# Six gate projections per layer as pairs by seven block products, and keys, queries and first transposes placed earlier, in a two-layer hybrid attention trunk

## The chip, the cores and the metric

The kernel runs on one core of a Trainium2 chip, in one launch. The metric is device time in microseconds (us) of one execution; lower is better. Three runs of the kernel before gave a median of 852.07 us (850.96 to 852.84). The profile used below is one further execution of the same program.

## The reference

The input is one sequence of 512 positions with 1024 channels, in fp32. Two layers follow each other; each computes

```
h = x @ w_in                      # 5024 columns: latents, gates, Diff q/k/v, merge gates
A: latent attention, 8 heads      # softmax(q k^T) v, times SiLU(gate_A), @ w_branch_a -> y_a
B: differential attention, 4 heads# (softmax1 - lam*softmax2) v, RMSNorm, times SiLU(gate_B), @ w_branch_b -> y_b
g = sigmoid(gates + b_merge)      # 2 x 1024 columns of h
merged = g[:, :1024] * y_a + g[:, 1024:] * y_b
x = LayerNorm(alpha * x + merged @ w_out)
```

So every layer has 16 merge gates of 128 columns each: eight for branch A and eight for branch B. A gate needs a product of a 128x1024 block of transposed weights with the whole transposed input (1024x512).

## The kernel before

**Layout and precision.** Almost everything is kept feature-major: 128 channels on the partitions, the 512 positions along the free axis. The input of a layer lies in SBUF as xH and xL: the value rounded to the matmul's format fp32r, and the remainder. Each weight tile is split likewise (`slot`, lines 109 to 116): one DMA of 128x1024 into a `wr` buffer, a cast on ACT to `wh` (line 112), and two subtractions on DVE to `wl` (line 115). A product of full precision is then three matmuls (`mm3`, lines 125 to 128): high by high, high by low, low by high. A projection (`proj`) is 8 blocks along the contraction, 24 matmuls of 512 columns in all, into one PSUM bank.

**Order of the work in a layer.** First come the latents and norms, then branch A's values (VS), then the eight heads of branch A. A head computes four blocks of scores (`mla_scores`), each followed on DVE by a row maximum (line 172) and on ACT by the exponential (line 174). The values of a head (`mla_values`) follow while the next head's scores run: `keyT` transposes a block of probabilities on PE (line 181, four matmuls against the identity), ACT casts the result from PSUM (line 183), DVE subtracts to get the low part (line 184), and two matmuls add to the output in the bank `pv` (lines 365, 366). `weave` alternates the two generators. Between heads stand `keys`, `query` and the projections of a table (`fill`, then `dfill` for branch B): SiLU gates, Diff q and k, Diff v. The four heads of branch B run in the same way. After the last matmul of a head's values comes a short chain: ACT copies the output to `op` (line 470), PE transposes it (line 476), ACT squares and sums it (line 479), two small DVE instructions (lines 481 and 482) prepare the variance, GpSimd raises it to the power -1/2 (line 484). The next step of that generator (the tail) broadcasts the result over the partitions by four transposes on PE (line 143, in `bcast`); DVE multiplies (lines 487, 488), and `split` makes the two parts of yB in `lat` buffers (lines 162, 163).

**The merge stage.** The eight A gates and A branch products are spread over heads 0 to 2 of branch B (`g` and `m` in `dfill`). After head 3 stand gate B0, the tail of head 3, and then four times two B gates and two B branch products (lines 590 to 601), and the output projection.

**What sets the order.** The kernel is written in program order, and a scheduler then places each engine's instructions by its own estimate of when each can start, so PE, ACT, DVE and the SP queue hold an order that mixes neighbouring steps. Every engine, and the SP queue that issues nearly all loads, works through its own list in that order. Buffers come from rings: two `wr`, three each of `wh` and `wl`, eight `p` (probabilities, and raw tiles), eight `y` (parts of yA), sixteen `qm`, two `op`, four `pt`, six `kv`. A write into a ring's buffer waits for the last reader of what lay there.

## Time and profile before

| what | value |
|---|---|
| median of three runs | 852.07 us (850.96 to 852.84) |
| the profiled execution, its own time | 851.0 us |
| span from its first to its last instruction | 849.1 us |
| granted TensorE clock, mean | 0.997 |
| PE busy | 837.6 us, 99% |
| DVE busy | 587.8 us, 69% |
| ACT busy | 428.0 us, 50% |
| GpSimd busy | 22.7 us, 3% |

PE is the matmul record, PEld the weight loads that run beside it. Matmul records overlap: one begins before the last has left the array, so that the distance from one start to the next, not the recorded duration, is what a matmul takes of PE's time. A row of the timeline reads: start in us, duration in us, engine, source line, operation, output and inputs, shape, count, and in brackets the idle time before it with what ended that.

### The profile page before, as it was taken

The page shows a single profiled execution, that of the slowest core. Times are in us where ns is not written, and L with a number is a line of the kernel's source. Part 1 is how long each engine was busy: PE and PEld are TensorE (multiplying, and loading weights), DVE is VectorE, ACT ScalarE, POOL GpSimd, SP SyncE. Part 2 cuts the span into 40 slices and gives each one's busy share as a digit, 9 for nine tenths or more (in the row PEclk, how much of TensorE's full clock was granted, in tenths as well). Part 3 has the DMA queues.
Part 4 walks back from the last instruction along what each step waited for, and adds up shares of the span by engine and source line. Part 5 has one row for each costly group of instructions (what it writes and reads, how often), then busy time and mean ns, then how long its engine had stood idle before and what let it go on. Part 6 is the DMA issues. An engine that isn't in the chain of part 4 may idle for free.

```text
span 849.1 us, 11080 instructions
## 1 busy us (share of the span) xinstructions
PE 837.6 (99%) x4143; PEld 695.7 (82%) x4143; DVE 587.8 (69%) x1070; ACT 428.0 (50%) x842; POOL 22.7 (3%) x30
## 2 busy tenths in 40 slices
PE   8999999999999999999999999999999999999996
PEld 7877877878898888888897778788788888888885
DVE  6789988586646845455867899877667566545457
ACT  5767775463544633332336777755546354433310
POOL 0100000000000000000120000000000000000001
PEclk9999999999999999999999999999999999999998
DMA  8311011213222452223532110112222233432322
GB/s 305 118 44 38 32 51 50 74 36 102 87 75 75 124 173 86 93 95 119 185 110 70 39 37 26 50 53 72 76 75 75 79 96 123 155 97 96 100 75 99
DMA packets 27702, 75.70 MB, mean 89 GB/s; under 512 B 3201, under 2 KB 7809, under 8 KB 27649
## 3 DMA queue, kind: packets, MB, share of 16 engines
q1 hardware_dynamic: 27504, 74.74, 27.7%
q8 instruction: 32, 0.52, 0.3%
q10 hardware_dynamic: 144, 0.26, 0.1%
q14 instruction: 22, 0.17, 0.1%
HBM read 70.80 MB, written 4.19 MB: 88 GB/s over the span
## 4 chain that ended last, share of the span: by engine, by line
PE 88%; ACT 5%; DVE 4%; DMA 2%; issue 1%; SPq 0%; POOL 0%; DVEq 0%; ACTq 0%
PE psacc L126 22%; PE psacc L127 22%; PE psacc L128 22%; PE pstr L181 4%; PE pspv L365 2%; PE pssc L126 2%; PE pssc L127 2%; PE pssc L128 2%; PE pspv L126 2%; PE pspv L366 2%; PE pspv L127 1%; PE pspv L128 1%; DMA wr<-in_wts_dram 1%; ACT wh L112 1%; PE pssc L444 1%; PE pssc L448 1%
## 5 line engine op out<-in xcount | busy, mean ns | idle before, releaser
L115 DVE TENSOR_TENSOR wl<-wr,wh 128x512 fp32r<-128x512 f32 x192 | 127.3, 686 | 145.6 <-ACT wh L112 145.2
L126 PE MATMUL psacc<-xH,wh 128*128 128x512 f32 x496 | 195.1, 393 | 0.0
L127 PE MATMUL psacc<-xL,wh 128*128 128x512 f32 x496 | 194.4, 392 | 0.0
L128 PE MATMUL psacc<-xH,wl 128*128 128x512 f32 x496 | 193.9, 391 | 0.0
L112 ACT CAST wh<-wr 128x1024 fp32r<-128x1024 f32 x96 | 101.0, 1052 | 175.0 <-PE psacc L127 115.5
L126 PEld LDWEIGHTS psacc<-xH,wh 128*128 128x128 f32 x496 | 93.2, 188 | 18.9
L127 PEld LDWEIGHTS psacc<-xL,wh 128*128 128x128 f32 x496 | 93.2, 188 | 18.4
L128 PEld LDWEIGHTS psacc<-xH,wl 128*128 128x128 f32 x496 | 93.2, 188 | 18.4
L174 ACT ACTIVATE p<-pssc,sm 128x512 f32<-128x512 f32 x128 | 88.2, 690 | 27.9 <-DVE sm L172 27.4
L172 DVE TENSOR_REDUCE sm<-pssc 128x1 f32<-128x512 f32 x128 | 86.7, 683 | 4.8 <-PE pssc L128 2.4
L183 ACT CAST pt<-pstr 128x512 fp32r<-128x512 f32 x96 | 55.6, 586 | 28.2 <-PE pstr L181 27.9
L184 DVE TENSOR_TENSOR pt<-pstr,pt 128x512 fp32r<-128x512 f32 x96 | 64.7, 685 | 7.1 <-ACT pt L183 6.3
L181 PE MATMUL pstr<-ident,p 128*128 128x128 f32 x384 | 57.3, 272 | 0.1
L181 PEld LDWEIGHTS pstr<-ident,p 128*128 128x128 f32 x384 | 47.3, 140 | 11.8 <-ACT p L174 0.5
L126 PE MATMUL psacc<-wh,xH 128*128 128x256 f32 x128 | 36.3, 284 | 0.0
L127 PE MATMUL psacc<-wl,xH 128*128 128x256 f32 x128 | 36.3, 284 | 0.0
L128 PE MATMUL psacc<-wh,xL 128*128 128x256 f32 x128 | 36.2, 283 | 0.0
L365 PE MATMUL pspv<-pt,vs 128*128 128x512 f32 x64 | 29.1, 455 | 0.4
L126 PE MATMUL pssc<-kv,qm 128*128 128x512 f32 x64 | 26.7, 423 | 0.9 <-ACT kv L306 0.6
L126 PE MATMUL psacc<-y,wh 128*128 128x512 f32 x64 | 25.5, 399 | 0.0
L366 PE MATMUL pspv<-pt,vs 128*128 128x512 f32 x64 | 25.5, 399 | 0.0
L127 PE MATMUL pssc<-kv,qm 128*128 128x512 f32 x64 | 25.3, 396 | 0.0
(296 smaller groups left out, 1591.6 us busy)
## 6 DMA issues: line engine op xcount, KB each, us to landing
wr<-in_wts_dram SPq DMA_DIRECT2D x106, 512.0 KB, 3.6
qr<-in_wts_dram SPq DMA_DIRECT2D x16, 128.0 KB, 2.1
p<-in_gb_dram SPq DMA_DIRECT2D x8, 256.0 KB, 2.9
y<-in_x_dram SPq DMA_DIRECT2D x8, 256.0 KB, 5.3
x_scratch<-y SPq DMA_DIRECT2D x8, 256.0 KB, 2.1
y<-x_scratch SPq DMA_DIRECT2D x8, 256.0 KB, 5.3
out_dram<-y SPq DMA_DIRECT2D x8, 256.0 KB, 2.0
p<-in_xT_dram SPq DMA_DIRECT2D x7, 256.0 KB, 4.9
```

The lines of the kernel that those rows point to most:

```text
L112: nc.scalar.copy(hi, raw)
L115: nc.vector.tensor_tensor(lo[:, c], raw[:, c], fr(hi[:, c]), ALU.subtract)
L126: nc.tensor.matmul(o, lhsT=lh, rhs=rh, start=start, stop=False)
L127: nc.tensor.matmul(o, lhsT=lh, rhs=rl, start=False, stop=False)
L128: nc.tensor.matmul(o, lhsT=ll, rhs=rh, start=False, stop=stop)
L172: nc.vector.tensor_reduce(m, S, axis=AX.X, op=ALU.max, negate=True)
L174: nc.scalar.activation(p, S, AF.Exp, bias=m, scale=1.0, accum_out=sums)
L181: nc.tensor.transpose(b[:, t * P:(t + 1) * P], pts[t][:, c * P:(c + 1) * P], ident)
L183: nc.scalar.copy(h, b)
L184: nc.vector.tensor_tensor(lo, b, fr(h), ALU.subtract)
L365: nc.tensor.matmul(pv, lhsT=v, rhs=ph, start=kc == 0, stop=False)
L366: nc.tensor.matmul(pv, lhsT=v, rhs=pl, start=False, stop=kc == NT - 1)
```

## The change

**Keys, queries and first transposes.** `mla_values` and `diff_values` gain a step at their start: the first `keyT` is issued, then the generator yields. The main loops take that step right after the scores of the head, ahead of `fill` and `dfill`. `keys` and `query` move from the start of a round to just after its `weave`, one head further ahead. The small computation of lambda moves from before the heads to behind the first scores.

**Gates B2 to B7.** They become three pairs, (2,3), (4,5) and (6,7). A pair is a product of a 256x1024 weight block with the 1024x512 input, cut into 2x2 blocks (128 by 512, and 512 by 256), and computed by seven block products with sums, in place of eight. A block product is 12 matmuls of 256 columns (`product`). The sums of the input's blocks are made once a layer on GpSimd (`x_forms`, four steps `x0` to `x3` in `dfill`), written to a DRAM tile `xf` by eight DMAs of GpSimd's queue, and loaded as four 128x1024 tiles through the `wr` ring (`y0` to `y3`, at the end of `dfill[2]`); each is split on ACT and DVE into two `y` or two `qm` pairs. The sums of the weights' blocks are four additions of 128x512 per pair on GpSimd (`add`), from four raw loads of 128x512 into `p` buffers; seven forms are split, each with a cast on ACT and a subtraction on DVE. `tc.issue_after` keeps the sums behind the latest power on GpSimd's list. Seven results are combined from PSUM by four ACT copies and three DVE additions of 256 columns, and the tanh moves behind these. The branch B products use the `sc` banks.

**The start.** Six instead of seven warming matmuls; the first block of the input is loaded in two pieces, both from SP's queue, with the first weights between them.

**How the order moves, place 1: the end of Diff head 3, PE and DVE.** On PE before (`pspv` is the output of head 3, `psacc_3214` gate B0, L476 the transposes of `op`):

```order
L126 MATMUL pspv_3130<-pt_3169,kv_2602 128x512
L127 MATMUL pspv_3130<-pt_3170,kv_2602 128x512
L128 MATMUL pspv_3130<-pt_3169,kv_2603 128x512
L126 MATMUL psacc_3214<-xH,wh_3209 128x512
L127 MATMUL psacc_3214<-xL,wh_3209 128x512
L128 MATMUL psacc_3214<-xH,wl_3210 128x512
L126 MATMUL psacc_3214<-xH,wh_3209 128x512
L476 MATMUL pstr_3193<-ident,op_3189 128x128 x4
L127 MATMUL psacc_3214<-xL,wh_3209 128x512
L128 MATMUL psacc_3214<-xH,wl_3210 128x512
```

PE now (L471 are the transposes of `op`, L144 the broadcast of the power, `psacc_3305` gate B0):

```order
L127 MATMUL pspv_3230<-pt_3260,kv_2662 128x512
L128 MATMUL pspv_3230<-pt_3261,kv_2662 128x512
L129 MATMUL pspv_3230<-pt_3260,kv_2663 128x512
L471 MATMUL pstr_3284<-ident,op_3280 128x128 x4
L144 MATMUL pstr_3332<-ident,sm_3296 128x128 x4
L127 MATMUL psacc_3305<-xH,wh_3300 128x512
L128 MATMUL psacc_3305<-xL,wh_3300 128x512
L129 MATMUL psacc_3305<-xH,wl_3301 128x512
```

Before, four matmuls of gate B0 stand between the values and the transposes, fourteen between the transposes and the broadcast (L143), and six more ahead of these among the values; now all 24 stand behind the broadcast. The same rows stand in the second layer.

On DVE before (L481 and L482 prepare the variance, L163 is the low part of head 2's yB, L487 multiplies by the broadcast, L115 is the low part of a weight tile):

```order
L481 SCALAR_TENSOR_TENSOR sm_3202<-s_448_1784 128x4
L163 TENSOR_TENSOR lat_3183<-op_2972,lat_3183 128x512
L482 SCALAR_TENSOR_TENSOR sm_3202<-sm_3192,sm_3202 128x4
L487 SCALAR_TENSOR_TENSOR g_3024<-pstr_3241,gs_477,g_3024 128x512
L115 TENSOR_TENSOR wl_3333<-wr_3330,wh_3332 128x512
L488 TENSOR_TENSOR op_3189<-op_3189,g_3024 128x512
```

DVE now (L476 and L477 prepare the variance, L164 is the low part of head 2's yB, L557 a form of a pair, L483 multiplies by the broadcast, and `wl_3301` belongs to gate B0):

```order
L476 SCALAR_TENSOR_TENSOR sm_3293<-s_130_592 128x4
L557 TENSOR_TENSOR pt_3409<-p_3378,pt_3408 128x512
L164 TENSOR_TENSOR lat_3274<-op_3023,lat_3274 128x512
L477 SCALAR_TENSOR_TENSOR sm_3293<-sm_3283,sm_3293 128x4
L557 TENSOR_TENSOR pt_3413<-p_3382,pt_3412 128x512
L483 SCALAR_TENSOR_TENSOR g_3084<-pstr_3332,gs_585,g_3084 128x512
L115 TENSOR_TENSOR wl_3301<-wr_3298,wh_3300 128x512 x2
```

The low part of gate B0's weights now stands behind the multiplication by the broadcast; before, only the later gates' weights did. On ACT the cast that L164 needs (`lat_3274`) stood ahead of the squares and now stands behind them.

**Place 2: the loads of the merge stage, SP and ACT.** SP before (`wr_3207` is gate B0, `p` are rows for the final norm, the two last are a branch B tile and a gate):

```order
L106 DMA wr_3082<-in_wts_dram 128x1024
L106 DMA wr_3207<-in_wts_dram 128x1024
L613 DMA p_3685<-in_gb_dram 128x512
L613 DMA p_3687<-in_gb_dram 128x512
L613 DMA p_3689<-in_gb_dram 128x512
L613 DMA p_3691<-in_gb_dram 128x512
L106 DMA wr_3251<-in_wts_dram 128x1024
```

SP now (`xf` are the second, third and fourth form of the input, `p` the raw weights of pair (4,5), `wr_3298` gate B0, `wr_3342` gate B1):

```order
L106 DMA wr_3200<-xf_90 128x1024
L106 DMA wr_3210<-xf_90 128x1024
L106 DMA wr_3220<-xf_90 128x1024
L546 DMA p_3560<-in_wts_dram 128x512
L546 DMA p_3562<-in_wts_dram 128x512
L546 DMA p_3564<-in_wts_dram 128x512
L546 DMA p_3566<-in_wts_dram 128x512
L106 DMA wr_3298<-in_wts_dram 128x1024
L106 DMA wr_3342<-in_wts_dram 128x1024
```

Gate B0's load now stands behind the loads of the forms, whose `wr` buffers it takes in turn, and behind raw weights that wait for the last transposes of head 3.

ACT before (L183 are casts of head 3's transposed blocks, L470 the copy of its output, L479 the squares):

```order
L183 CAST pt_3136<-pstr_3131 128x512
L183 CAST pt_3145<-pstr_3140 128x512
L183 CAST pt_3157<-pstr_3152 128x512
L183 CAST pt_3169<-pstr_3164 128x512
L470 COPY op_3189<-pspv_3130 128x512
L162 CAST lat_3183<-op_2972 128x512
L479 ACTIVATE tmp_3191,sm_3192<-pstr_3193 128x128 x4
```

ACT now (L163 and L166 split the forms, L184 are the casts of transposed blocks, L465 the copy, L474 the squares):

```order
L166 ACTIVATE y_3206<-wr_3200 128x512
L184 CAST pt_3236<-pstr_3231 128x512
L184 CAST pt_3248<-pstr_3243 128x512
L163 CAST qm_3212<-wr_3210 128x512
L184 CAST pt_3260<-pstr_3255 128x512
L163 CAST qm_3216<-wr_3210 128x512
L556 CAST pt_3408<-p_3378 128x512
L163 CAST qm_3222<-wr_3220 128x512
L465 COPY op_3280<-pspv_3230 128x512
L163 CAST qm_3226<-wr_3220 128x512
L474 ACTIVATE tmp_3282,sm_3283<-pstr_3284 128x128 x4
L163 CAST lat_3274<-op_3023 128x512
```

The cast of head 3's last transposed block now stands behind the split of the third form, and the copy of its output behind that of the fourth.

**The diff**, cut to its core (layout on the host, the moved lambda lines and the start are left out where the text says all):

```diff
         def mla_values(h, pts):
             c, e = h // 2, h % 2
+            nxt = keyT(pts, 0)
+            yield
             pv = pt_("pv")
-            nxt = keyT(pts, 0)
...
-        def diff_values(h, pts, v, g, s1):
+        def diff_values(h, pts, s1):
+            nxt = keyT(pts, 0)
+            yield
             pv = pt_("pv")
-            nxt = keyT(pts, 0)
...
                 o = (kc % 2) * 256 + (h % 2) * P
-                vh, vl = v[kc // 2]
+                vh, vl = vd[h // 2][kc // 2]
...
-            nc.gpsimd.tensor_tensor(r, e, mhalf[:, 0:4], ALU.pow)
+            pows[h] = nc.gpsimd.tensor_tensor(r, e, mhalf[:, 0:4], ALU.pow)
             yield
...
-            acc = pt_("acc")
+            acc = pt_("sc" if which else "acc")
...
+        def x_forms(j):
+            ra, rb, f, g = (t2("qm") for _ in range(4))
+            for v, k in ((ra, j), (rb, j + 4)):
+                nc.gpsimd.tensor_tensor(v, fr(xH[:, k, :]), fr(xL[:, k, :]), ALU.add)
+            nc.gpsimd.tensor_tensor(f[:, c1], ra[:, c1], ra[:, c2], ALU.subtract)
+            nc.gpsimd.tensor_tensor(f[:, c2], f[:, c1], rb[:, c2], ALU.add)
+            nc.gpsimd.tensor_tensor(g[:, c1], rb[:, c2], ra[:, c2], ALU.subtract)
+            nc.gpsimd.tensor_tensor(g[:, c2], f[:, c2], rb[:, c1], ALU.subtract)
+            for i, v in ((0, f), (2, g)):
+                nc.gpsimd.dma_start(xf[:, i:i + 2, j * 256:(j + 1) * 256], v.rearrange("p (a b) -> p a b", a=2))
+        def load_x_form(i):
+            raw = load(xf[:, i, :])
+            out = []
+            for o in (0, 512):
+                h, lo = split(raw[:, o:o + 512], "y" if i < 2 else "qm", -1.0 if i == 1 else None)
+                out += [(h[:, c], lo[:, c]) for c in (c1, c2)]
+            XF.append(out)
+        def gate_pair(c):
+            i = SLOTS.index(f"gtB{c}")
+            G = wts[l, i:i + 2].rearrange("s (q r) n -> (s q) (r n)", r=2)
+            raw = []
+            for i in range(4):
+                raw.append(t2("p"))
+                nc.sync.dma_start(raw[i], G[:, i * 512:(i + 1) * 512])
+            r11, r12, r21, r22 = raw
+            def add(a, b):
+                o = t2("kv")
+                nc.gpsimd.tensor_tensor(o, a, b, ALU.add)
+                return o
+            def form(v, room):
+                hi, lo = room
+                nc.scalar.copy(hi, v)
+                nc.vector.tensor_tensor(lo, v, fr(hi), ALU.subtract)
+                return room
+            def halves():
+                h, lo = t2("wh", F32R, 1024), t2("wl", F32R, 1024)
+                return [(h[:, o:o + 512], lo[:, o:o + 512]) for o in (0, 512)]
...
+            with tc.issue_after(pows[3].ins) if c == 2 else nullcontext():
+                f3 = add(r11, r21)
+                f1 = add(r21, r22)
+                f2 = add(f3, r22)
+                f4 = add(f2, r12)
+                a, b = halves()
+                W11 = form(r11, a)
+                F1 = form(f1, b)
+                a, b = halves()
+                F2 = form(f2, a)
+                F4 = form(f4, b)
+                F3 = form(f3, two("op"))
+                W12 = form(r12, two("pt"))
+                W22 = form(r22, two("pt"))
+
...
+            def product(o, w, xs_, first):
+                for k in range(4):
+                    (wh, wl), (h, lo) = (v[:, k * P:(k + 1) * P] for v in w), xs_[k]
+                    for n, (a, b) in enumerate(((wh, h), (wh, lo), (wl, h))):
+                        nc.tensor.matmul(o, lhsT=a, rhs=b, start=first and k == 0 and n == 0,
+                                         stop=k == 3 and n == 2, skip_group_check=True)
+            tag = "g" if c == 4 else "qw"
+            t0, t1 = t2(tag), t2(tag)
+            Y, Z, X = (pt_("acc")[:, c1] for _ in range(3))
+            product(Y, W11, block(0, 0), True)
+            nc.scalar.copy(t0[:, c1], Y)
+            product(Z, F1, XF[0], True)
+            nc.scalar.copy(t1[:, c1], Z)
+            product(Y, F2, XF[1], False)
+            nc.scalar.copy(t0[:, c2], Y)
+            product(Z, F4, block(1, 1), False)
+            nc.vector.tensor_tensor(t0[:, c2], Z, t0[:, c2], ALU.add)
+            product(Y, F3, XF[2], False)
+            nc.scalar.copy(t1[:, c2], Y)
+            product(X, W12, block(1, 0), True)
+            nc.vector.tensor_tensor(t0[:, c1], X, t0[:, c1], ALU.add)
+            nc.vector.tensor_tensor(t1[:, c2], t1[:, c2], t1[:, c1], ALU.add)
+            col = 8 + c
+            nc.scalar.activation(t0, t0, AF.Tanh, bias=bh[:, col:col + 1], scale=0.5)
+            product(Y, W22, XF[3], False)
+            nc.scalar.activation(t1[:, c2], t1[:, c2], AF.Tanh, bias=bh[:, col + 1:col + 2], scale=-0.5)
+            nc.scalar.activation(t1[:, c1], Y, AF.Tanh, bias=bh[:, col + 1:col + 2], scale=-0.5)
+            return t0, t1
...
+                elif f[0] == "x":
+                    with tc.issue_after(pows[max(pows)].ins):
+                        x_forms(i)
+                elif f[0] == "y":
+                    load_x_form(i)
...
-        fill = {0: ["q0"], 1: ["k0"], 2: [], 3: ["q1"], 4: ["k1", "a2"], 5: [], 6: ["a3"], 7: []}
+        fill = {0: ["q0"], 1: ["k0"], 2: [], 3: ["q1"], 4: ["k1", "a2"], 5: [], 6: ["a3"], 7: ["b0", "v0"]}
         ps_ = {0: weave(mla_scores(0, q.pop(0)))}
...
         for h in range(8):
-            if h % 2 == 1 and h < 7:
-                keys(h // 2 + 1)
-            if h < 6:
-                q[h + 2] = query(h + 2)
             if h < 7:
-                ps_[h + 1] = weave(mla_scores(h + 1, q.pop(h + 1)), mla_values(h, ps_.pop(h)))
+                ps_[h + 1] = weave(mla_scores(h + 1, q.pop(h + 1)), val)
+                if h % 2 == 0 and h < 6:
+                    keys(h // 2 + 1)
+                if h < 5:
+                    q[h + 3] = query(h + 3)
+                val = mla_values(h + 1, ps_.pop(h + 1))
+                next(val)
             else:
-                weave(mla_values(h, ps_.pop(h)))
+                weave(val)
             run(fill[h])
         dfill = {
-            0: ["g0", "m0", "g1", "m1", "b1", "q2", "k2", "g2", "m2", "g3", "m3"],
-            1: ["v1", "b2", "q3", "k3", "g4", "m4", "g5", "m5"],
-            2: ["b3", "g6", "m6", "g7", "m7"],
+            0: ["x0", "x1", "g0", "m0", "g1", "m1", "b1", "q2", "k2", "g2", "m2", "g3", "m3"],
+            1: ["x2", "x3", "v1", "b2", "q3", "k3", "g4", "m4", "g5", "m5"],
+            2: ["b3", "g6", "m6", "g7", "m7", "y0", "y1", "y2", "y3"],
             3: [],
         }
         ps_ = {0: weave(diff_scores(0, qd.pop(0), kd.pop(0), s1[0]))}
         tail = None
+        val = diff_values(0, ps_.pop(0), s1[0])
+        next(val)
         for h in range(4):
-            val = diff_values(h, ps_.pop(h), vd[h // 2], gB[h], s1[h])
             gens = [diff_scores(h + 1, qd.pop(h + 1), kd.pop(h + 1), s1[h + 1])] if h < 3 else []
             for i in range(5):
...
             tail = val
+            if h < 3:
+                val = diff_values(h + 1, ps_.pop(h + 1), s1[h + 1])
+                next(val)
             run(dfill[h])
         hold["B0"] = gate(1, 0)
         next(tail)
         merged = []
-        for c2 in range(4):
-            ths = [gate(1, 2 * c2) if c2 else hold.pop("B0"), gate(1, 2 * c2 + 1)]
-            for i in range(2):
-                c = 2 * c2 + i
-                acc = branch(1, c, yB)
-                th = ths[i]
-                nc.vector.scalar_tensor_tensor(th, th, 1.0, acc, ALU.add, ALU.mult)
-                nc.vector.tensor_tensor(th, th, mA[c // 2][:, i * 512:i * 512 + 512], ALU.add)
-                merged.append(split(th, "qm", 0.5))
+        ths = [hold.pop("B0"), gate(1, 1)]
+        for c in range(8):
+            if c in (0, 2, 4):
+                ths += gate_pair(c + 2)
+            acc = branch(1, c, yB)
+            th = ths[c]
+            nc.vector.scalar_tensor_tensor(th, th, 1.0, acc, ALU.add, ALU.mult)
+            nc.vector.tensor_tensor(th, th, mA[c // 2][:, (c % 2) * 512:(c % 2) * 512 + 512], ALU.add)
+            merged.append(split(th, "qm", 0.5))
```

More of the change, by code (lines that the diff above doesn't have):

```diff
@@ L1 @@
 import math
-from contextlib import ExitStack
+from contextlib import ExitStack, nullcontext
 import numpy as np
@@ L41 @@
     + ["vd10", "vd11", "gb2", "qd3", "kd3", "gtA4", "brA2", "gtA5", "gb3", "gtA6", "brA3", "gtA7"]
[1 row of a table removed]
+    + ["gtB0", "gtB1", "brB0", "brB1", "brB2", "brB3"] + [f"gtB{c}" for c in range(2, 8)]
     + [f"o{n}{k}" for n in range(2) for k in range(4)]
@@ L94, in hybrid_trunk @@
     warm = pt_("sc")
-    for i in range(7):
+    for i in range(6):
         nc.tensor.matmul(warm, lhsT=zero[:, 0:P], rhs=zero, start=True, stop=True)
@@ L116, in slot, with load_x @@
         return hi, lo
-    def load_x(k):
-        raw = t2("p")
-        (nc.scalar if k == 0 else nc.sync).dma_start(raw, xT[:, k * SEQ:(k + 1) * SEQ])
-        nc.scalar.copy(xH[:, k, :], raw)
-        nc.vector.tensor_tensor(xL[:, k, :], raw, fr(xH[:, k, :]), ALU.subtract)
+    def load_x(k, cols=slice(0, SEQ), raw=None):
+        raw = t2("p") if raw is None else raw
+        nc.sync.dma_start(raw[:, cols], xT[:, k * SEQ + cols.start:k * SEQ + cols.stop])
+        nc.scalar.copy(xH[:, k, cols], raw[:, cols])
+        nc.vector.tensor_tensor(xL[:, k, cols], raw[:, cols], fr(xH[:, k, cols]), ALU.subtract)
+        return raw
     def mm3(o, lh, ll, rh, rl, start, stop):
@@ L187, in layer @@
     def layer(l, last):
+        xf = dram.tile([P, 4, 1024], F32, name=f"xf{l}")
         pr = prms[:, l, :]
@@ L209, in layer @@
         for k in range(KC):
[L210 to L212 removed]
+            if l + k == 0:
+                first = load_x(0, slice(0, P))
+                load_wc(0)
+                load_x(0, slice(P, SEQ), first)
+            else:
+                if l == 0:
+                    load_x(k)
+                load_wc(k)
             if l == 0:
@@ L706, in _pack @@
         c = int(s[-1]) if s[-1].isdigit() else 0
+        if s in ("gtB3", "gtB5", "gtB7"):
+            continue
+        if s in ("gtB2", "gtB4", "gtB6"):
+            o = O_GT + DM + c * P
+            a = np.concatenate([_fm(w_in, o + i * P + r(P)).reshape(P, DM) for i in range(2)], 1)
+            outs += list(a.reshape(2, P, 1024))
+            continue
         if s.startswith("vd"):
```

47 lines of the change are left out of this document (27 added, 20 removed), and 1 row of the table SLOTS.

## The prediction

> **What bounds the kernel now.** I read the page's totals and chain first, then the starts of single matmuls, then the waits of PE, then the end of Diff head 3 row by row. On the page, the second line is each engine's busy time, the third the chain that ended last, the last two are groups of matmuls with their mean duration in ns behind the comma.
>
> ```profile
> span 849.1 us, 11080 instructions
> PE 837.6 (99%) x4143; PEld 695.7 (82%) x4143; DVE 587.8 (69%) x1070; ACT 428.0 (50%) x842; POOL 22.7 (3%) x30
> PE 88%; ACT 5%; DVE 4%; DMA 2%; issue 1%; SPq 0%; POOL 0%; DVEq 0%; ACTq 0%
> L126 PE MATMUL psacc<-xH,wh 128*128 128x512 f32 x496 | 195.1, 393 | 0.0
> L126 PE MATMUL psacc<-wh,xH 128*128 128x256 f32 x128 | 36.3, 284 | 0.0
> ```
>
> PE is the bound: less matmul time shortens the kernel, and any new stop of PE lengthens it. Records overlap, so the pitch from start to start is the price. These rows begin and end two unbroken stretches, one of 512 and one of 256 columns (start us, duration us):
>
> ```profile
> 319.80 0.39 PE L128 MATMUL psacc<-xH,wl 128*128 128x512 f32 x1
> 329.78 0.39 PE L127 MATMUL psacc<-xL,wh 128*128 128x512 f32 x1
> 148.55 0.28 PE L126 MATMUL psacc<-wh,xH 128*128 128x256 f32 x1
> 159.93 0.28 PE L128 MATMUL psacc<-wh,xL 128*128 128x256 f32 x1
> ```
>
> 44 pitches lie in the first, 9.98 / 44 = 0.2268 us; 95 in the second, 11.38 / 95 = 0.1198 us. Half the columns take 0.53 of the time. What PE still waits for is small (view of waits: who, for whom, us in all, times, us each; then a stretch of the A heads, with busy us and counts of PE, PEld, DVE, ACT, GpSimd, then clock and DMA):
>
> ```profile
> PEld pspv L365 <- ACT pt L183: 4.9, 16, 0.6
> PEld pspv L126 <- ACT pt L183: 2.6, 8, 0.5
> PEld pssc L126 <- ACT p L174: 2.0, 7, 0.6
> PEld pssc L126 <- ACT kv L306: 1.5, 2, 0.8
> 64.00:106.00 42.00, 41.89 (x209) 33.55 (x209) 40.59 (x72) 30.76 (x63) 0.00 (x0) 1.00 0.11 35
> ```
>
> The first two are the first values of each head, which wait for the head's first transposed block: 7.5 us in 24 waits.
>
> **The change, part by part.** *Products.* A pair of gates is 48 matmuls of 512 columns now, 48 x 0.2268 = 10.89 us. As a pair by seven products it is 84 of 256, 84 x 0.1198 = 10.06 us: 0.83 us less, and for three pairs in two layers **-4.9 us**. The sums must be hidden for that. A product is 12 x 0.1198 = 1.44 us. The stage offers this room:
>
> ```profile
> 320.00:390.00 70.00, 70.00 (x310) 57.98 (x309) 34.27 (x53) 23.34 (x29) 0.00 (x0) 1.00 0.32 99
> 1.01 0.29 POOL masks.py:199 TENSOR_SCALAR_AFFINE_SELECT ident<-ident 128x128 f32<-128x128 f32 x1
> ```
>
> DVE is busy for 34.27 and ACT for 23.34 of 70 us, so that copies and sums of 256 columns between products fit. GpSimd adds 128x512: its only row of width is 0.29 us for 128x128, which scaled gives an estimate of 1.16 us; four of them stand behind head 3's power, against 24 x 0.2268 x 2 = 10.9 us of gates B0 and B1 before the first pair. I price this at 0. If an addition should take three times that, 13.9 us, the excess of 3.0 us shows once per layer: 0 to +6. The forms of the input stand on GpSimd's list between the powers of different heads, which are tens of us apart, and their DMAs go through GpSimd's own queue: 0.
>
> *Keys, queries, first transposes.* At most all of the waits go: 7.5 + 2.0 + 1.5 = 11.0 us. But the order gives DVE not one instruction less, and in the stretch of the A heads DVE has 1.41 us left of 42, with PE beside it. A transposed block that is ready earlier moves the wait to the row maxima of the next scores. I take a third, **-3.6**, with 0 and -11.0 as bounds. The moved steps issue the same loads from the same queue, and the lambda step is a handful of small instructions: 0.
>
> *The start.* (start, duration; in brackets the idle time before, and for what)
>
> ```profile
> 1.22 3.17 PE L96 MATMUL pssc<-p 128*128 128x512 bf16 x7 [1.22 <-DVE p L93]
> 4.87 0.62 ACT L122 CAST xH<-p 128x512 fp32r<-128x512 f32 x1 [2.42 <-DMA p<-in_xT_dram]
> 5.54 0.46 PE L126 MATMUL psacc<-kv,xH 128*128 128x416 f32 x1 [1.16 <-ACT xH L122]
> ```
>
> The first real matmul waits for a cast of 0.62 us of 512 columns; a piece of 128 takes part of that. One warm-up fewer lies in a gap of 1.16 us. I take **-0.3**, between -1 and +1.
>
> *The end of Diff head 3.* This is the large term. Today it reads, in the first layer:
>
> ```profile
> 304.15 0.39 PE L126 MATMUL psacc<-y,wh 128*128 128x512 f32 x1
> 313.40 0.39 PE L128 MATMUL pspv<-pt,kv 128*128 128x512 f32 x1
> 313.83 0.59 ACT L470 COPY op<-pspv 128x512 f32<-128x512 f32 x1 [1.54 <-PE pspv L128]
> 314.56 0.60 PE L476 MATMUL pstr<-ident,op 128*128 128x128 f32 x4
> 314.65 0.62 ACT L162 CAST lat<-op 128x512 fp32r<-128x512 f32 x1 [0.23 <-DVE op L488]
> 315.30 0.69 DVE L163 TENSOR_TENSOR lat<-op,lat 128x512 fp32r<-128x512 f32 x1 [0.61 <-ACT lat L162]
> 316.46 0.16 DVE L482 SCALAR_TENSOR_TENSOR sm<-sm,sm 128x4 f32<-128x4 f32 x1 [0.46 <-ACT tmp L479]
> 316.70 1.01 POOL L484 TENSOR_TENSOR sm<-sm,mhalf 128x4 f32<-128x4 f32 x1 [25.20 <-DVE sm L482]
> 318.20 0.60 PE L143 MATMUL pstr<-ident,sm 128*128 128x128 f32 x4
> 318.56 0.48 PE L126 MATMUL psacc<-xH,wh 128*128 128x512 f32 x1
> 318.84 0.75 DVE L487 SCALAR_TENSOR_TENSOR g<-pstr,gs,g 128x512 f32<-128x512 f32 x1 [2.22 <-PE pstr L143]
> 319.51 0.68 DVE L115 TENSOR_TENSOR wl<-wr,wh 128x512 fp32r<-128x512 f32 x1
> ```
>
> From the values' last matmul (313.40) to the end of the power (317.71) are 4.31 us, and PE does not notice, since gate B0 runs underneath: it starts gate B1 at 318.56. In the new order all of gate B0 stands behind the broadcast, which needs the power, and PE works strictly through its list. Per layer:
>
> (a) The chain itself lies open: 4.31, less 0.23 for the values' last matmul and 0.36 for the transposes that PE does within it, **3.7**.
>
> (b) The cast of head 2's yB (0.62) now stands on ACT behind the squares, and its low part (0.69) still stands on DVE ahead of the last small instruction, which so waits for both: **+1.3**.
>
> (c) The low part of gate B0's weights stands on DVE behind the multiplication by the broadcast, and the third matmul of the gate needs it. Today the multiplication starts 0.64 after the broadcast's first transpose (318.20) and takes 0.75, the subtraction 0.68, 2.07 together; the broadcast (318.56 - 318.20 = 0.36) and the gate's first two matmuls (0.45) cover part: **+1.2**.
>
> (d) The cast of head 3's last transposed block stands on ACT behind the split of the input's third form, and that form's load behind the release of both `wr` buffers and of the `y` buffers that the branch matmuls of 304.15 read. The load is issued some 2.8 us after that start, and a load of this size takes
>
> ```profile
> DMA to landing us min/median/max: 2.4/3.5/5.7
> ```
>
> so it lands at about 310.4, and its first half is through ACT and DVE some 1.3 us after the transposed block could have been cast: **+1.3**, between 0 and 2.5. (e) Half of the fourth form's split delays the copy to `op`: **+0.45**.
>
> Together 7.95 us in each layer, **+15.9 us**; with (a) alone 7.4 us.
>
> *The clock.* The two rows are the stretches after the kernel's last matmul, which ends at 842.2:
>
> ```profile
> 842.20:844.40 2.20, 0.01 (x1) 0.00 (x0) 2.05 (x6) 0.00 (x0) 0.63 (x1) 1.00 0.18 68
> 844.60:849.00 4.40, 0.00 (x0) 0.00 (x0) 1.67 (x3) 0.00 (x0) 0.08 (x1) 0.50 0.32 119
> ```
>
> The granted clock (third last) is 1.00 for 2.2 us and 0.50 thereafter. In the new order the chain from the values to the power is 4.31 + 1.31 = 5.6 us; the transposes end 314.56 + 0.60 - 313.40 = 1.8 us into it, which leaves PE 3.8 us with nothing, and after four transposes come the 1.2 us of (c). So the clock is likely to fall in it. At the start of the kernel the warm-ups take 3.17 / 7 = 0.45 us each, twice the pitch above, and all of them do; 3.2 us of work at half rate cost 1.6 us, **+3.2 us** for two layers, between 0 and that. [...]
>
> **The sum.** The profiled execution took 851.0 us by its own time (span 849.1), 1.07 below the median of the runs, 852.07. 851.0 - 4.9 - 3.6 - 0.3 + 15.9 + 3.2 = 861.3.
>
> **The rivals.** (A) *Faster.* Only the open chain (a) costs, the detours (b) to (e) and the clock do not, and the waits of PE go entirely: 851.0 - 4.9 - 11.0 - 0.3 + 7.4 = **842.2**. For it: the waits are short, 0.5 to 0.6 us each, and the orders of ACT and DVE need not bind if loads land early. Against it: DVE at 40.59 of 42.
>
> (A') *The same.* Detours as above, waits gone, the clock holds: 851.0 - 4.9 - 11.0 - 0.3 + 15.9 = **850.7**.
>
> (B) *Slower still.* The loads become the chain: two `wr` buffers carry three forms and gate B0 one after the other, gate B0's load also behind raw weights that wait for head 3's last transposes. If the form and gate B0's tile each take the longest landing, 5.7 instead of 3.5, that is 4.4 us per layer, 8.8 more: **870.1**. It decides from the point at which gate B0's tile lands after the broadcast; by my timeline it lands about 2 us before.
>
> (C) *The products do not shrink.* Were the recorded 284 ns the price, 84 x 0.284 = 23.9 against 48 x 0.393 = 18.9 us, +30 us in six pairs. The pitches contradict it.
>
> **How the numbers follow.** Forecast 0.60, A 0.15, A' 0.11, B 0.13, C 0.01. 0.2% is 1.7 us, about what a measurement of this kernel can tell from no change. A is faster; A' is within; the others are slower: faster 0.15, same 0.11, slower 0.74. Predicted 861. The forecast's own bounds are 861.3 - 3.2 (no clock) - 2.6 (d at 0) - 3 (more of the waits) = 852.5 below; to hold A' the range goes to 850, above to B, 871. Left out are A and C, 0.16, and a little of the ends.
>
> **What would show it.** Right: in the trace after, PE idle between the transposes of head 3's output and the broadcast in both layers, 4 to 6 us each, ended by GpSimd's power; gate B0's third matmul waiting for DVE; the `pt` waits present in part; pair matmuls at a pitch of 0.12 us; a granted clock below 1 around gate B0. Wrong: that gap at 4 us or less and no first-transposes waits (A), or a PE wait for a `wr` load or for ACT's split of a form (B). Terms (d) and (e) do not exist if no matmul of head 3's values waits for ACT's cast of the last transposed block.

## The result, and the profile after

The changed kernel takes 879.84 us (median of 4 runs, 878.65 to 880.1) against 851.52 us (4 runs, 850.56 to 852.84): ratio 1.033, interval 1.0314 to 1.0346. The forecast was 861, with a range up to 871: right in sign, and too small by 19 us. The profile after, page lines and the matmul group that answers to the first group of before:

```profile
span 878.3 us, 11853 instructions
PE 846.2 (96%) x4358; PEld 704.9 (80%) x4358; DVE 648.6 (74%) x1123; ACT 457.0 (52%) x919; POOL 124.2 (14%) x118
PE 85%; ACT 6%; DVE 5%; DMA 2%; issue 1%; POOL 1%; SPq 0%; DVEq 0%; POOLq 0%; ACTq 0%
L127 PE MATMUL psacc<-xH,wh 128*128 128x512 f32 x400 | 160.2, 401 | 0.0
```

PE was idle for 849.1 - 837.6 = 11.5 us, now for 32.1. It was also busy 8.6 us longer, although the pairs save matmul time: part of the work ran at a granted clock of 0.50, as shown below. DVE is busy 60.8 us longer for 53 instructions more.

**Where the time lies.** A stage is the distance between the starts of the same matmuls in the two timelines, in us.

| stage | before | after | difference |
|---|---|---|---|
| to the first score of branch B, layer 1 | 160.05 | 162.87 | +2.8 |
| to the last value matmul of head 3 | 153.35 | 154.28 | +0.9 |
| merge: to the first output projection | 86.87 | 96.98 | +10.1 |
| to the first score of branch B, layer 2 | 179.46 | 180.45 | +1.0 |
| to the last value matmul of head 3 | 153.39 | 155.48 | +2.1 |
| merge | 86.86 | 97.73 | +10.9 |
| to the last matmul | 21.95 | 21.95 | 0.0 |

The stages follow each other without a gap. The sum is 27.8 us; the 1.4 us that remain of the spans lie behind the last matmul and were not looked into. Most of the loss lies in the two merge stages, but they are not alone, and they contain the gain of the products.

The view of waits of the changed kernel (who, for whom, us, times, longest):

```profile
PE pstr L144 <- POOL sm L479: 8.0, 2, 4.0
PE pstr L471 <- ACT op L465: 4.0, 2, 2.3
PE psacc L129 <- DVE wl L115: 2.1, 2, 1.1
PEld pssc L127 <- ACT p L175: 6.7, 16, 1.0
PEld pstr L182 <- ACT p L175: 4.8, 11, 0.5
PEld pspv L359 <- ACT pt L184: 2.9, 12, 0.4
```

The first three rows are the forecast gap, once in each layer: the broadcast waits for the power, the transposes for the copy, gate B0's third matmul for DVE. The last three stand in the heads: the wait on the first transposed block of branch A shrank from 4.9 to 2.9 us, as the change means it to, but scores (6.7 us, before 2.0) and transposes (4.8, before 0.5) now wait more for ACT's exponentials.

The end of head 3 in the first layer, row by row from PE, ACT, DVE and GpSimd:

```profile
317.14 0.40 PE L129 MATMUL pspv<-pt,kv 128*128 128x512 f32 x1
318.08 0.62 ACT L163 CAST qm<-wr 128x512 fp32r<-128x512 f32 x1 [1.13 <-DMA wr<-xf]
318.60 0.58 ACT L465 COPY op<-pspv 128x512 f32<-128x512 f32 x1
319.23 1.12 PE L471 MATMUL pstr<-ident,op 128*128 128x128 f32 x4 [1.69 <-ACT op L465]
321.31 0.22 ACT L474 ACTIVATION_READ_ACCUMULATOR tmp<-pstr 128x1 f32 x1
322.06 0.69 DVE L164 TENSOR_TENSOR lat<-op,lat 128x512 fp32r<-128x512 f32 x1 [0.77 <-ACT lat L163]
322.67 0.15 DVE L477 SCALAR_TENSOR_TENSOR sm<-sm,sm 128x4 f32<-128x4 f32 x1
322.97 1.32 POOL L479 TENSOR_TENSOR sm<-sm,mhalf 128x4 f32<-128x4 f32 x1 [28.68 <-DVE sm L477]
324.35 1.11 PE L144 MATMUL pstr<-ident,sm 128*128 128x128 f32 x4 [4.00 <-POOL sm L479]
326.17 2.84 DVE L115 TENSOR_TENSOR wl<-wr,wh 128x512 fp32r<-128x512 f32 x2
324.27 2.50 POOL L551 TENSOR_TENSOR kv<-p,p 128x512 f32<-128x512 f32 x2
326.73 1.73 POOL L551 TENSOR_TENSOR kv<-kv,p 128x512 f32<-128x512 f32 x1
327.37 0.80 PE L129 MATMUL psacc<-xH,wl 128*128 128x512 f32 x1 [1.06 <-DVE wl L115]
```

The fourth form lands at about 318.08, after ACT has waited 1.13 us for it, and the cast of its first half stands ahead of the copy; the low part of head 2's yB stands ahead of the last small instruction; the low parts of gate B0 stand behind the broadcast. The last rows hold something the prediction did not have: the two subtractions take 1.15 and 1.77 us (together 2.84, since the records overlap), against 0.68 before, while GpSimd adds.

The granted clock (third last column) around that stretch, then the start of the kernel:

```profile
316.50:318.50 2.00, 0.73 (x2) 0.30 (x2) 1.51 (x3) 0.87 (x2) 0.00 (x0) 1.00 0.83 245
318.50:332.00 13.50, 7.71 (x21) 5.62 (x22) 10.43 (x13) 7.63 (x19) 8.95 (x7) 0.50 0.53 169
332.00:334.00 2.00, 2.00 (x10) 1.64 (x9) 2.00 (x2) 0.00 (x0) 1.54 (x1) 0.96 0.79 291
3.86 0.71 PE L127 MATMUL psacc<-kv,xH 128*128 128x416 f32 x1
4.72 0.35 PE L129 MATMUL psacc<-kv,xL 128*128 128x416 f32 x1
6.04 0.46 PE L127 MATMUL psacc<-kv,xH 128*128 128x416 f32 x1 [0.97 <-ACT xH L122]
```

In windows of half a microsecond the fall lies at 318.52 and the rise at 332.18, so half clock lasts 13.66 us. PE's transposes, the broadcast and more than half of gate B0 fall into it. The start is 5.54 - 3.86 = 1.68 us earlier, and then waits for the second piece.

The products themselves do what was said. The pair (4,5) reaches from its first product to the branch matmul that follows:

```profile
355.69 0.28 PE L591 MATMUL psacc<-xH,wh 128*128 128x256 f32 x1
365.76 0.40 PE L127 MATMUL pssc<-lat,wh 128*128 128x512 f32 x1
```

That is 10.07 us, where 10.06 was worked out; the other five pairs take 10.07 or 10.18.

### The profile page after: what moved, and what is told of

Same layout as the page of the kernel before. It is cut to its first block, busy times and chain, and to the rows that moved or that the text cites. A ratio compares the mean times of both kernels' runs of the same rounds, so it can differ in the third digit from the quotient of the medians.

```text
span 878.3 us, 11853 instructions
## 1 busy us (share of the span) xinstructions
PE 846.2 (96%) x4358; PEld 704.9 (80%) x4358; DVE 648.6 (74%) x1123; ACT 457.0 (52%) x919; POOL 124.2 (14%) x118
## 4 chain that ended last, share of the span: by engine, by line
PE 85%; ACT 6%; DVE 5%; DMA 2%; issue 1%; POOL 1%; SPq 0%; DVEq 0%; POOLq 0%; ACTq 0%
PE psacc L129 17%; PE psacc L127 17%; PE psacc L128 17%; PE psacc L591 7%; PE pstr L182 4%; PE pssc L127 4%; PE pssc L128 3%; PE pssc L129 3%; ACT p L175 2%; PE pspv L359 2%; PE pspv L360 2%; PE pspv L127 1%; PE pspv L129 1%; PE pspv L128 1%; DMA wr<-xf 1%
## 5 line engine op out<-in xcount | busy, mean ns | idle before, releaser
L115 DVE TENSOR_TENSOR wl<-wr,wh 128x512 fp32r<-128x512 f32 x168 | 133.5, 816 | 82.7 <-ACT wh L112 82.6
L129 PE MATMUL psacc<-xH,wl 128*128 128x512 f32 x400 | 159.0, 397 | 2.1 <-DVE wl L115 2.1
L127 PE MATMUL psacc<-xH,wh 128*128 128x512 f32 x400 | 160.2, 401 | 0.0
L128 PE MATMUL psacc<-xL,wh 128*128 128x512 f32 x400 | 159.1, 398 | 0.0
L112 ACT CAST wh<-wr 128x1024 fp32r<-128x1024 f32 x84 | 88.3, 1051 | 114.5 <-PE psacc L128 57.8
L129 PEld LDWEIGHTS psacc<-xH,wl 128*128 128x128 f32 x400 | 76.2, 191 | 18.7 <-DVE wl L115 3.6
L128 PEld LDWEIGHTS psacc<-xL,wh 128*128 128x128 f32 x400 | 76.9, 192 | 15.2
L127 PEld LDWEIGHTS psacc<-xH,wh 128*128 128x128 f32 x400 | 76.8, 192 | 14.9
L479 POOL TENSOR_TENSOR sm<-sm,mhalf 128x4 f32<-128x4 f32 x8 | 8.8, 1099 | 522.6 <-PE psacc L129 323.5
L184 ACT CAST pt<-pstr 128x512 fp32r<-128x512 f32 x96 | 55.6, 586 | 23.8 <-PE pstr L182 23.1
L786 POOL TENSOR_TENSOR sm<-sm,mhalf 128x1 f32<-128x1 f32 x8 | 7.9, 993 | 174.8 <-DVE sm L785 174.8
L127 PE MATMUL pssc<-kv,qm 128*128 128x512 f32 x64 | 27.6, 432 | 1.8 <-ACT p L175 1.8
```

The lines of the kernel that those rows point to most:

```text
L112: nc.scalar.copy(hi, raw)
L115: nc.vector.tensor_tensor(lo[:, c], raw[:, c], fr(hi[:, c]), ALU.subtract)
L127: nc.tensor.matmul(o, lhsT=lh, rhs=rh, start=start, stop=False)
L128: nc.tensor.matmul(o, lhsT=lh, rhs=rl, start=False, stop=False)
L129: nc.tensor.matmul(o, lhsT=ll, rhs=rh, start=False, stop=stop)
L184: nc.scalar.copy(h, b)
```

## The experiments

Each ran three rounds against the kernel before, whose median was 852.2 to 852.4 in them. Ratios are to the kernel before. Differences to the change compare runs of different times, between which the median of the kernel before moved by 0.9 us at most (851.5 to 852.4).

**e1: the reorder alone.** In the kernel before, `keys`, `query` and the first `keyT` are moved as in the change, with the lambda step; gates and start stay.

```diff
-            if h % 2 == 1 and h < 7:
-                keys(h // 2 + 1)
-            if h < 6:
-                q[h + 2] = query(h + 2)
...
+                val = mla_values(h + 1, ps_.pop(h + 1))
+                next(val)
```

> The kernel before with the earlier keys, queries and first transposes alone; gates, forms and start as before. Theory 1 (the step of the prediction that failed is the gain of 3.6 us: the A heads are paced by DVE and ACT, and PE, reaching transposes and scores sooner, only waits more): 853 to 857 us, with waits of score matmuls and first transposes on ACT's exponential (L174) where waits on the transposed block stood. Theory 2 (the reorder itself gains as forecast, and the slower A heads of the changed kernel come from the pairs, through buffers, queues or GpSimd): 845 to 850 us. Theory 3 (neither): 851 to 852.

Measured: 855.79 against 852.4 us, ratio 1.0039 (1.0026 to 1.0052). Theory 1. Its waits are those of the changed kernel, almost to the tenth:

```profile
PEld pssc L126 <- ACT p L174: 6.7, 16, 1.0
PEld pstr L181 <- ACT p L174: 4.8, 11, 0.5
PEld pspv L351 <- ACT pt L183: 3.0, 12, 0.4
```

**e2: the pairs alone.** The reverse: all of `x_forms`, `load_x_form` and `gate_pair`, with the old loops and the old start.

> The kernel before with the three pairs and the sums alone; keys, queries, first transposes and start as before. Theory 1 (the loss is at the end of Diff head 3, and comes with the loads of the input's forms, not with the reorder): about 852 - 5 + 27 = 872 to 876 us. Theory 2 (the loss at head 3 needs the reorder too, since the first transposes of head 3 now stand ahead of the last projections): 846 to 852 us.

Measured: 870.16 us, ratio 1.021 (1.0195 to 1.0225), below the 872 to 876 of theory 1 and far above theory 2. The gap at head 3 needs no reorder. But e1 and e2 add up to 21 us, and the change loses 28. Part of what the reorder adds to the pairs is seen in DVE's rows at the end of head 3:

```profile
319.63 0.16 DVE L484 SCALAR_TENSOR_TENSOR sm<-sm,sm 128x4 f32<-128x4 f32 x1 [0.18 <-ACT tmp L481]
320.13 0.69 DVE L164 TENSOR_TENSOR lat<-op,lat 128x512 fp32r<-128x512 f32 x1 [0.34 <-ACT lat L163]
321.00:328.00 7.00, 5.94 (x16) 4.42 (x17) 5.93 (x5) 3.27 (x6) 6.92 (x5) 0.51 0.28 82
```

Without the reorder, the small instruction stands ahead of the low part. From the values' last matmul to the broadcast pass 4.6 and 4.7 us in the two layers, in the change 7.2 and 7.8, and half clock lasts 6.8 us in the first layer and 10.2 in the second, in the change 13.7 in both.

**e3: the forms' loads behind gate B1.** One line of the changed kernel is moved.

```diff
-            2: ["b3", "g6", "m6", "g7", "m7", "y0", "y1", "y2", "y3"],
+            2: ["b3", "g6", "m6", "g7", "m7"],
...
         ths = [hold.pop("B0"), gate(1, 1)]
+        run(["y0", "y1", "y2", "y3"])
```

> The changed kernel with one line moved: the four loads of the input's forms stand behind gate B1 instead of behind the last A branch product, so that gate B0 can stand under head 3's chain again (16 of its 24 matmuls between the transposes and the broadcast in PE's list). Theory 1 (all of the 13.5 and 15.4 us that the two merge entries lost come from gate B0 standing behind the broadcast, by the open chain, the casts of forms in ACT's list and the clock): 852 to 856 us. Theory 2 (the forms' loads and splits cost the same elsewhere, now ahead of the first pair): 865 to 880 us. The gap between head 3's transposes and broadcast then has no idle PE and the granted clock stays at 1.00.

Measured: 868.31 us, ratio 1.0192 (1.0174 to 1.021): 11.5 us less than the change, and 12 us more than theory 1 allows; it is in the range of theory 2. The gap is gone, as this stretch shows (PE busy 12.00 of 12, clock 1.00). In its place the first pairs wait:

```profile
318.00:330.00 12.00, 12.00 (x59) 9.74 (x59) 9.70 (x15) 7.24 (x20) 7.77 (x6) 1.00 0.68 224
PE psacc L591 <- ACT g L598: 4.3, 2, 2.1
PE psacc L591 <- DVE op L557: 1.9, 2, 1.0
```

A product waits for an ACT copy of an earlier result. In the first layer (351.68) that copy stands in ACT's list behind the split of merged columns (350.21), for which ACT had itself waited 1.71 us on DVE, and DVE's subtractions of two SBUF operands, which take up to 1.78 us in the change, stand ahead of it. So the place of the loads is only part of the loss; DVE is late as well.

**e4: keep PE busy in the gap.** 24 matmuls per layer, whose result nobody reads, are added to the changed kernel.

```diff
         hold["B0"] = gate(1, 0)
+        keep = pt_("sc")
+        for i in range(24):
+            nc.tensor.matmul(keep, lhsT=xH[:, i % 8, 0:P], rhs=xH[:, i % 8, :], start=True, stop=True)
         next(tail)
```

> The changed kernel with 24 more matmuls of 512 columns per layer, whose result nobody reads, in the idle stretch around head 3's last transposes (15 of them, 3.4 us, between the transposes and the broadcast, 4 ahead of the transposes). They only keep PE busy where it idles. Theory 1 (half rate after the gap costs 3.6 to 4.1 us per layer: every matmul of gate B0 starts 0.43 instead of 0.23 us after the one before): 871 to 873 us, 7 to 8.5 less, and the granted clock stays at 1.00 between head 3 and gate B1. Theory 2 (the clock costs 1.6 us per layer as forecast): 876 to 877. Theory 3 (gate B0 is held by DVE's low parts and the clock costs nothing): 879 to 881.

Measured: 870.2 us, ratio 1.0222 (1.0202 to 1.0241): with 48 matmuls more, the kernel is 9.6 us faster than the change. The clock stays at 1.00 through the place where it had been 0.50:

```profile
317.00:332.00 15.00, 13.12 (x58) 9.86 (x59) 12.98 (x18) 9.09 (x22) 8.23 (x6) 1.00 0.60 187
```

The 9.6 us are not the clock alone, since the edit moved other lists too: ACT's cast of head 2's yB now stands between the squares, DVE's low parts of gate B0 stand ahead of the multiplication by the broadcast, and in the second layer the fourth form lands 1.1 us earlier relative to the values. What the clock itself costs can be read from parts that have the same order in both traces: gate B0's third to last matmul take 7.1 us in the change and 4.9 here, from the first transpose to the first square 1.15 and 0.69, and from the broadcast to its multiplication 1.15 in the change and 0.64 before. Together that is an estimate of 3.2 us per layer, twice the forecast 1.6.

**e5 and e6: the two halves of the reorder.** In e5 only the first transposes are early; in e6 only `keys` and `query`.

> The kernel before with the first transposes of each head ahead of the work between heads, and the lambda step moved; keys and queries stay at the start of a round. Theory 1 (the loss of 3.4 us of the whole reorder comes from PE standing at transposes whose probabilities ACT hasn't written yet, with the other work queued behind them): 853 to 856 us. Theory 2 (the loss comes from the keys and queries, whose scores then run ahead of ACT's exponentials): 850 to 852.

> The kernel before with keys and queries moved to the end of the round before; first transposes as before. Theory 1 (the transposes are the loss): 850 to 852.5 us. Theory 2 (keys and queries are): 853 to 857.

Measured: e5 854.07 us, 1.0022 (1.0012 to 1.0032), within theory 1; e6 860.5 us, 1.0104 (1.0087 to 1.012), more than its theory 2 allowed. Neither half gains, and together they lose less than keys and queries alone. In e6 the old waits on first blocks double, and the scores wait too:

```profile
PEld pspv L365 <- ACT pt L183: 10.3, 24, 1.9
PEld pssc L126 <- ACT p L174: 9.1, 18, 1.0
```

Why e6 loses so much is not shown. The head number in the call is one higher, but in program order `keys` and `query` only change places with the projections of `fill`: the same work lies between two rounds of scores as before.

**e7: additions on GpSimd that nobody reads.** 42 per layer in the kernel before, in the loop over the heads of branch A. The scheduler starts them early: they run from 29.4 to 92.9 us in the first layer, the first score stands at 56.1.

```diff
+        idle = t2("qm")
         for h in range(8):
+            for _ in range(6 if h < 7 else 0):
+                nc.gpsimd.tensor_tensor(idle, tabs[:, 1, :], tabs[:, 2, :], ALU.add)
```

> The kernel before with 42 additions of 128x512 per layer on GpSimd during the heads of branch A, whose result nobody reads; PE, ACT and DVE have their old lists. Theory 1 (an addition on GpSimd doubles the time of those DVE instructions that read two operands from SBUF, 0.69 to 1.4 us and more, as beside the pairs' sums): about 16 us of such work per layer become 30, in a stretch in which DVE has few us to spare, so 860 to 880 us. Theory 2 (GpSimd's sums cost the others nothing, as the prediction had it): 851 to 853.

Measured: 883.44 us, ratio 1.0375 (1.0356 to 1.0394), 31 us for work on an engine that was 97% idle, more than theory 1 allowed. Its groups, with the mean in ns behind the comma:

```profile
L562 POOL TENSOR_TENSOR qm<-tabs 128x512 f32<-128x512 f32 x84 | 120.4, 1434 | 6.4
L163 DVE TENSOR_TENSOR qm<-tmp,qm 128x512 fp32r<-128x512 f32 x16 | 15.1, 945 | 0.8 <-ACT qm L162 0.7
L184 DVE TENSOR_TENSOR pt<-pstr,pt 128x512 fp32r<-128x512 f32 x96 | 64.7, 684 | 7.5 <-ACT pt L183 6.9
```

The instruction with two operands in SBUF (L163) rises from 683 to 945 ns in the mean of its 16 executions, and one of 256 columns (L315) from 412 to 904. The ones that read an operand from PSUM stay: L184 at 684, L396 at 681. The trace of the change shows the same, execution by execution: of DVE's instructions of 128x512 with two operands in SBUF, the 32 that begin while an addition or subtraction on GpSimd has 0.29 us or more to run take 0.84 to 1.78 us, and five that begin less than 0.08 us before its end take 0.67 to 0.68; ten that read an operand from PSUM, and begin beside 0.29 us or more, take 0.67 to 0.75. The 31 us hold a second cost: PE had to wait for DVE (7.3 us in four waits at L366 alone), and the mean granted clock was 0.991, before 0.997.

**e8: the pairs alone, placed late.** e2 with the forms' loads behind gate B1 and more branch products ahead of the pairs.

```diff
-            if c in (0, 2, 4):
-                ths += gate_pair(c + 2)
+            if c in (2, 3, 4):
+                ths += gate_pair(2 * c - 2)
```

> The kernel before with the pairs, but with the four loads of the input's forms behind gate B1 and the pairs behind two, three and four branch B products (instead of 0, 2 and 4); keys, queries, transposes and start as before. Theory 1 (what the pairs lose is only their place: gate B0 fills the gap again, and two branch products more cover the forms and sums of the first pair): 846 to 852 us. Theory 2 (forms and sums cost more than the 4.9 us that the products save wherever they stand, since DVE slows down beside GpSimd and ACT's list is long): 855 to 868.

Measured: 863.96 us, ratio 1.0144 (1.0124 to 1.0163). Theory 2. Its waits are at DVE's low parts and ACT's copies:

```profile
PE pssc L129 <- DVE wl L115: 4.0, 2, 2.0
PE psacc L598 <- ACT qw L605: 3.7, 2, 2.4
PE psacc L598 <- ACT qw L607: 1.8, 2, 0.9
```

**e9 and e10: the sums of weights on DVE.** One word is changed, in the changed kernel (e9) and in e8 (e10).

```diff
-                nc.gpsimd.tensor_tensor(o, a, b, ALU.add)
+                nc.vector.tensor_tensor(o, a, b, ALU.add)
```

> The changed kernel with the twelve sums of weights per layer on DVE (0.69 us each by the nearest row) instead of GpSimd; the forms of the input stay on GpSimd, all else as in the change. Theory 1 (beside an addition on GpSimd a DVE instruction with two operands in SBUF takes 1.4 to 1.8 us, and gate B0's low parts stand under the first four additions, so this is part of the loss at the merge entry): 875 to 878 us, and the third matmul of gate B0 waits 0.7 us less per layer. Theory 2 (it is hidden by the half clock of that stretch, and four additions of 0.69 in DVE's list ahead of head 3's small instructions cost as much): 879 to 882.

> As the late pairs (forms behind gate B1, pairs behind two, three and four branch products, no reorder), with the sums of weights on DVE. Theory 1 (of the 11.8 us that the late pairs lose, the waits on DVE's low parts beside GpSimd's additions are some 2.2 us per layer, and ACT's copies behind form splits 2.5 per layer remain): 857 to 861 us. Theory 2 (the additions only move): 863 to 866.

Measured: e9 873.23 us, 1.0246 (1.0226 to 1.0266), 6.6 less than the change; e10 851.7 against 852.43 us, 0.9996 (0.9986 to 1.0006), 12.3 less than e8, and more than theory 1 forecast in both. Giving DVE 24 instructions more of 0.69 us made the kernel faster: in e10 the three waits of e8 shown above are gone altogether. The low part of a form takes 692 ns in e10, where the changed kernel had 929; first e10, then the changed kernel:

```profile
L564 DVE TENSOR_TENSOR wl<-kv,wh 128x512 fp32r<-128x512 f32 x18 | 12.1, 692 | 0.4
```

```profile
L557 DVE TENSOR_TENSOR wl<-kv,wh 128x512 fp32r<-128x512 f32 x18 | 16.2, 929 | 0.8
```

Neither run separates two effects. The low parts of the forms no longer stand beside a sum on GpSimd (692 ns in e10), and the sums are also ready sooner: 0.69 us each, against 1.51 and 1.58 in the mean on GpSimd. That the first effect exists is shown by e7 (683 to 945 ns), in which nobody waits for a sum.

**e11: two pairs only.** e10 with B2 and B3 as plain gates again.

> Only gates (4,5) and (6,7) as pairs; B2 and B3 as before, so that 24 + 24 + 24 + 24 matmuls and two branch products lie between head 3 and the first pair; forms behind gate B1, sums of weights on DVE, no reorder. The products save 4 x 0.83 = 3.3 us. Theory 1 (with enough PE work ahead, ACT and DVE hide the forms): 848 to 852 us. Theory 2 (the forms cost PE waits wherever they stand): 854 to 860.

Measured: 853.52 us, ratio 1.0016 (1.0007 to 1.0026), at the edge between the two theories: more cover ahead of the pairs brings nothing, since e10 has no such wait left.

**e12: the start alone.**

> The kernel before with the new start alone (six warming matmuls, first block of the input in two pieces on one queue). Theory 1 (the first real matmul is 1.7 us earlier but the third waits 1.1 us for the second piece, as in the trace of the change): 851 to 852 us, a gain of 0.3 to 1. Theory 2 (one warming matmul fewer lets the clock rise later, and the start loses): 852.5 to 854.

Measured: 851.74 us, ratio 1.0001 (0.9992 to 1.0011): within theory 1's range, but no difference that can be told from none. Its first matmul starts as early as in the change (3.83 us), but the first ones follow each other at 0.52 us.

No version beats the kernel before by more than its measurement is uncertain. In e10 the merge stages are 1.7 and 1.5 us shorter than before, of 2.5 that the products save, and the stretch ahead of them 0.9 longer in each layer, with one matmul more of gate B0 in it; what makes the rest of that stretch longer was not tried. Its profile also has a slower start than that of the kernel before: the first 12 real matmuls (416 columns) follow each other at 0.35 us instead of 0.19, which puts the last matmul of that kind 1.8 us later. In the profiles this happens with the old start (e1 and e2 have 7 and 8 matmuls from 6 to 8 us, the kernel before 12) and the new (e3 has 6), and the 25 runs of the kernel before beside e10 lie in two groups, 850.8 to 851.4 and 852.0 to 853.3. Leaving the start out, e10's trace is 1.1 us shorter than that of before.

## Why the prediction was right or wrong

Three terms failed: the reorder's gain had the wrong sign, the sums on GpSimd had no price, and half clock cost twice what was forecast. The products came out as forecast, and so, but for one step, did the chain at head 3.

**Right: the products.** 10.07 us for a pair, 10.06 forecast.

**Right: gate B0 behind the broadcast, steps (a) to (e).** In both layers PE stands idle for 4.0 us between the transposes and the broadcast, and the power ends it, as forecast. The steps, in the first layer: (d) from the first matmul of the last A branch product to the values' last are 9.1 us (308.05 to 317.14). Before they were 9.25, of which six matmuls of gate B0 took 1.36, so it is 1.2 us longer, forecast 1.3. (b) was 322.67 - 321.53 = 1.14, forecast 1.3. (c) was a wait of 1.06 with PE at half rate (granted clock 0.50), forecast 1.2. (e) was 1.0 instead of 0.45, and 1.6 in the second layer: ACT first waited for the fourth form to land and then cast half of it, where the forecast had only half a split. The broadcast came 7.2 and 7.8 us after the values' last matmul.

**Wrong in size: "3.2 us of work at half rate cost 1.6 us".** The forecast let the clock come back when PE had worked for as long as at the start of the kernel. It came back 332.18 - 327.37 = 4.8 us after gate B0's third matmul, and fell already 1.0 us after the values' last matmul had ended (318.52). So the transposes, the broadcast and more than half of gate B0 ran at half rate (from its fourth on, the gate's matmuls start 0.43 us apart up to 331.81, and 0.23 after the rise), about 3.2 us per layer by the rows of e4, 6.4 instead of 3.2. Both stretches of half clock in the change last 13.65 us, four times 3.41, and in each layer PE's records fill 0.33, 0.29, 0.69 and 1.00 of the four parts: the part filled to 0.69 did not bring the clock back. Nor did the fall come after an idle part: PE was busy for 1.71 of the 3.41 us before it, and for 1.23 in the second layer. The 3.41 us before the fall, and those before the rise:

```profile
315.11:318.52 3.41, 1.71 (x8) 0.72 (x6) 2.55 (x4) 2.28 (x5) 0.00 (x0) 1.00 0.81 238
328.76:332.18 3.42, 3.42 (x9) 2.64 (x8) 3.42 (x3) 1.14 (x2) 3.42 (x3) 0.50 0.58 154
```

**Wrong in sign: "I take a third, -3.6".** The bounds held no loss, and e1 shows one of 3.4 us. The upper bound of 11.0 was too large as well: it was read from waits of weight loads (PEld). By the distances from start to start, PE itself lost 3.2 us ahead of the 24 first value matmuls before, not 7.5. e1 brings that to 0.5, so the step did what it was meant to; but by the same reckoning PE now loses 3.3 us ahead of transposes, where it had lost 0.2, and scores wait more too. The failed step is the assumption that a wait could only shrink or move on: transposes placed earlier wait for exponentials that ACT has not written, and hold up the work behind them. For keys and queries (e6) the cause stays open.

**Wrong: "I price this at 0", the sums on GpSimd.** The price was looked for in GpSimd's own time. It lies in DVE's: in the change a DVE instruction of 128x512 that reads two operands from SBUF and begins beside an addition on GpSimd takes up to 1.78 us, where the kernel before has 0.63 to 0.75 for such instructions. e7 shows the effect without any pair (683 to 945 ns in the mean). Moving the weight sums to DVE gains 6.6 us in the change (e9) and 12.3 us with the pairs placed late (e10); these sizes include that the sums are ready sooner.

**No difference: the start.** -0.3 was forecast, and e12 cannot tell it from nothing.

With what the runs showed in place of the three terms, 861.3 + (3.6 + 3.4) + 6.6 + (6.4 - 3.2) = 878.1 us, against 880.1 of the profiled execution. The parts overlap: the mean granted clock of e9 is 0.987, that of the change 0.983, so its 6.6 hold some of the clock's cost, and e1 and e2 do not add up to the change. So this nearness is no proof of each.

## What to carry to other kernels

Price an edit on an idle engine by what it does to its neighbours: a look for a DVE instruction with two SBUF operands beside it (here up to 1.78 us instead of 0.68) costs nothing, and moving the GpSimd additions away gained 6.6 and 12.3 us here, more than the 4.9 that the products save. A gap on PE cost its length and then the half-rate work behind it, here some 3 us on top of a gap of 7 to 8; work that nobody needs was cheaper than the gap (9.6 us in e4). Where ACT and DVE pace a stage, placing PE's work earlier can move its waits and add to them (3.4 us in e1). And read a wait of PE from the distances of its matmuls: those of the weight loads promised twice as much as PE lost.

## What the runs showed of the hardware

- In the change a DVE instruction of 128x512 with two operands in SBUF takes 0.84 to 1.78 us when it begins while an addition or subtraction on GpSimd has 0.29 us or more to run (32 executions), and 0.67 to 0.68 when it begins less than 0.08 us before the end of one (five). Four that begin while GpSimd issues DMAs (L528) take 1.66 to 2.81. With none of these at their start they take 0.64 to 0.75, and so did all of them in the kernel before (0.63 to 0.75). Those that read an operand from PSUM take 0.67 to 0.75 beside an addition, too. GpSimd's own addition of 128x512 takes 1.41 to 1.58 us in the mean in the change and 1.43 in e7, not the 1.16 that scaling gave.
- In the traces of the kernel before and of the change the granted clock changes only at steps of 3.41 us, counted from its first record (4.83 and 4.50 us): it is at 1.00 for 246 steps before, and in the change for 92, 123 and 32, with four steps of 0.50 between them each time. PE's records fill 0.33 of the step ahead of the fall in the kernel before, and 0.50, 0.36 and 0 of those ahead of the three falls in the change; the clock stayed up through 489 other steps, none filled less than 0.57. In the change it rose both times after a full step, and stayed at 0.50 through six filled 0.29 to 0.69. In the two merge entries of the change it fell 1.0 and 1.6 us after the values' last matmul had ended, with shorter waits of PE ahead of that.
- The first real matmuls of the kernel run slower in some profiles than in others. In the kernel before, those of 416 columns follow each other at 0.19 us from about 6 us on, and 12 of them fall into the 2 us from 6 to 8; in e1, with the same start, it is 7, and 9 from 8 to 10. What sets this was not shown.
